# Block transposes through device memory: four loads and a store per tensor, and two more tensors by the same way

## The chip, the cores and the metric

The kernel runs on one core of a Trainium2 chip. The metric is the device time of one execution in microseconds; the kernel before takes 1913.64 us (median of three runs, 1913.54 to 1913.78).

## The reference, cut to what matters

A decoder trunk of two layers on a residual stream x of 256 positions by 2048 channels, all in float32.

- Layer 0: RMS norm, one projection to 12288 + 4096 columns, then 16 heads of stick-breaking attention and 16 heads of dilated attention (head dimension 128, sequence 256), a SiLU gate, and an output projection 4096 to 2048 that is added to x.
- Layer 1: RMS norm, one projection to 16384 columns (q, forget, input, gate), 32 HGRN heads with a 128 x 128 state in chunks, an RMS norm of each head's output, a SiLU gate, and an output projection.

```
a = where(mask, exp(log_sigmoid(z) + tail), 0)            # stick-breaking weights, [queries, keys]
out = a @ v
p = exp(sc - lse);  o = p @ v                             # dilated attention, three strides merged
o = rms_norm(hgrn2(q, f, i, lb), o_gain) * silu(gate)     # HGRN head
x = x + mix @ w_out
```

For the work around the change one thing counts: attention weights come out with queries on the 128 partitions and are needed with keys there, and a HGRN head's output comes out with positions on the partitions and is needed with channels there. Both are transposes.

## The kernel before

**The stream of weights.** All the weights are cut into 640 parts of 128 x 2 x 512 floats (512 KB). Each goes: SP issues a load into a `raw` tile (`Feed.load`, L227, four buffers); ScalarE rounds it to `whi` (L244); VectorE takes the rest, `wlo` (L245); TensorE multiplies 12 times with it (L287 to L289: for two column blocks and two halves of the sequence, `whi` by the activations' high part, `wlo` by the high part, `whi` by the low part). `whi` and `wlo` have four buffers each. A head of either layer takes 8 parts (96 of these weight matmuls), the output projection of a layer 64 parts.

**The heads beside it.** `Side` (L256) holds one generator per head. After each of the 16 steps of a product it advances the generators; `yield n` asks to be called again n steps later. So a head's own work (transposes, scores, softmax, gates) is written into the stream of weights some steps after its product, and lies between the weight matmuls of the next heads.

**What sets the order.** The program is not run in the order in which it is written: a scheduler orders each engine's instructions before the run, by its own costs and by when it takes their inputs to be ready. Each engine then works strictly through its own list. The order rows below are those lists.

**Transposes.** Three kinds stand in the kernel before:
- q, k (and the gate in layer 0), `turn` (L157): `move_blocks` (L143) sends the 4 x 4 blocks of 32 partitions in 16 transfers from the tile `qkp` to the tile `mvp`, each from one group of 32 partitions to another; then one VectorE instruction (L171) transposes all the 32 x 32 blocks. The last head of each layer uses TensorE in place of this (`quick`).
- attention weights, `flip_weights` (L178): three TensorE transposes (`flip`, L136, L140) into a PSUM tile `att`, and a ScalarE copy (L182) to `atk`.
- HGRN outputs (L582): two TensorE transposes into PSUM, read from there by `finish` (L336), which writes the high part (`mixh`, ScalarE, L131) and the low part (`mixl`, VectorE, L132).

**A head of layer 0, step by step**, with the lines that the prediction names: q, k, v and gate are copied from the accumulators (L315, L321); q, k and gate are turned (L171); in a dilated head ScalarE scales k (L411); the gate is computed by VectorE (L327), ScalarE's exponential (L328), VectorE (L329), a reciprocal (L330) and a product (L331); TensorE makes the scores (`products`, L361, L362). A stick-breaking head reads them on VectorE (L371), passes three ScalarE functions (L375 to L377), then VectorE (L378), two scans (L382) and a difference (L383), and ScalarE's exponential (L384). A dilated head reads them with two masked maxima (L420), then has ScalarE's exponentials (L426), sums (L429) and the division (L435). The weights are transposed, TensorE multiplies them by v (`values_by_weights`, L354, L355), VectorE multiplies by the gate (L388 or L439), and `finish` follows.

Of the kernel before, what the change touches and what calls it, by code (L numbers as in the profile page):

```python
# [10 lines left out]
F32 = mybir.dt.float32  # L11
# [20 lines left out]
SG = 4  # L32
# [3 lines left out]
def hybrid_trunk(  # L36
# [23 lines left out]
    psa = ctx.enter_context(tc.tile_pool(name="psa", bufs=4, space=bass.MemoryType.PSUM))  # L60
    psb = ctx.enter_context(tc.tile_pool(name="psb", bufs=4, space=bass.MemoryType.PSUM))
# [74 lines left out]
    def flip(blocks):  # L136

        ps = psb.tile([P, len(blocks) * P], F32, name="att")
        for i, b in enumerate(blocks):
            nc.tensor.transpose(ps[:, i * P : (i + 1) * P], b, ident)  # L140
        return ps

    def move_blocks(moved, src):  # L143


        for a in range(4):
            for b in range(4):
                nc.sync.dma_start(
                    *(
                        v.rearrange("p c t j -> p (c t j)")  # L150
                        for v in (moved[32 * b : 32 * b + 32, a], src[32 * a : 32 * a + 32, b])
                    )
                )
                if b % 2:
                    yield 1

    def turn(flat, part, quick):  # L157


        n = part.shape[2]  # L160
        out = flat.rearrange("p (c t) -> p c t", c=n)
        if quick:
            ps = [flip([part[:, :, c, t, :] for t in range(NT)]) for c in range(n)]
            for c in range(n):
                nc.scalar.copy(out[:, c, :], ps[c])
        else:
            moved = work.tile([P, 4, n, NT, 32], F32, name="mvp", bufs=1)
            yield 2
            yield from move_blocks(moved, part)
            yield 3  # L170
            nc.vector.transpose(  # L171
                out.rearrange("p c (t a j) -> p a (c t) j", t=NT, a=4),
                moved.rearrange("p a c t j -> p a (c t) j"),
            )
            yield 1
        return out

    def flip_weights(w):  # L178

        ps = flip([w[:, j * P : (j + 1) * P] for j in range(3)])  # L180
        at = work.tile([P, 384], F32, name="atk", bufs=2)
        nc.scalar.copy(at, ps)  # L182
        return at
# [181 lines left out]
    def stick_breaking(h, flat, part, v):  # L365
# [18 lines left out]
        nc.scalar.activation(z, z, AF.Exp)  # L384
        yield 12
        at = flip_weights(z)
        yield 3
# [4 lines left out]
    def dilated(h, flat, part, v):  # L392
# [41 lines left out]
        for t in range(NT):  # L434
            nc.vector.tensor_scalar_mul(pr[:, spans[t]], pr[:, spans[t]], ws[:, t : t + 1])  # L435
        yield 8
        at = flip_weights(pr)
        yield 3
# [4 lines left out]
    def blocks(a, n):  # L443
        return a.rearrange("p (b n) -> p b n", n=n)

    def hgrn(h, flat, part, vg):
# [43 lines left out]
        tots = work.tile([P, 2, nb], F32, name="tots")  # L490
# [32 lines left out]
        mm = work.tile([P, 8, 6], F32, name="mm")  # L523
        pr = work.tile([P, 8, 2], F32, name="pr")
# [28 lines left out]
        mx = work.tile([P, 6], F32, name="mx")  # L553
        pr = work.tile([P, 4], F32, name="px")
# [21 lines left out]
        yield 4  # L576
        for t in range(NT):
            nc.vector.scalar_tensor_tensor(
                sg[:, t, :], o[:, t, :], ro[:, t : t + 1], sg[:, t, :], op0=ALU.mult, op1=ALU.mult
            )  # L580
        yield 2
        finish(h, flip([sg[:, t, :] for t in range(NT)]), hg[:, 2:3])  # L582
# [166 lines left out]
```

## Time and profile before

| | |
|---|---|
| median of 3 runs | 1913.64 us |
| the profiled execution | 1914.46 us |
| its span, first to last instruction | 1912.7 us |
| TensorE matmul busy | 1903.1 us (100%) |
| VectorE busy | 1317.7 us (69%) |
| ScalarE busy | 1055.2 us (55%) |
| DMA queue of SP | 144752 packets, 363.11 MB, 60.3% of 16 engines |

The spans of matmuls overlap, so a matmul's cost is read from the distance of the starts around it, not from its duration. The profiled execution lies 0.82 us above the median, and its span 1.76 us below its own time. An engine's idle time matters only where TensorE then waits for it.

### The profile page before, as it was taken

To read this page: it belongs to the slowest core of one execution; us is meant where nothing else is said; L and a number is where in the kernel's file an instruction comes from. 1 tells how busy PE (TensorE), PEld (TensorE's weight loads), DVE (VectorE), ACT (ScalarE), POOL (GpSimd) and SP (SyncE) were. 2 spreads that over 40 slices of the span, in tenths; PEclk is the share of its full clock that TensorE was granted. 3 is DMA by queue.
4 is the path that set the end of the run, shared out by engine and by line. 5 is a ranking of instruction groups with operands and counts; after the bars stand their busy time and mean duration, and the time that the engine had idled before them with its cause. 6 is when DMAs were issued, how large, how long until landed. Compare 5 with 4: busy or idle time off the path is not lost.

```text
span 1912.7 us, 26414 instructions
## 1 busy us (share of the span) xinstructions
PE 1903.1 (100%) x8778; PEld 1586.0 (83%) x8778; DVE 1317.7 (69%) x2598; ACT 1055.2 (55%) x1882; POOL 42.0 (2%) x54
## 2 busy tenths in 40 slices
PE   8999999999999999999999999999999999999999
PEld 7888888888888888888888888888888888888887
DVE  6667777766666666655567777777777777777443
ACT  6555555555555555544456566555565555555332
POOL 0000000000000000000000000000000000000000
PEclk9999999999999999999999999999999999999999
DMA  8666666666666666555565555556555565655664
GB/s 317 197 213 197 198 197 193 196 199 193 194 195 200 195 195 200 177 188 188 187 199 181 182 181 176 174 183 184 172 183 186 178 185 177 186 177 165 198 206 136
DMA packets 145034, 364.82 MB, mean 191 GB/s; under 512 B 27008, under 2 KB 59904, under 8 KB 144896
## 3 DMA queue, kind: packets, MB, share of 16 engines
q1 hardware_dynamic: 144752, 363.11, 60.3%
q8 instruction: 69, 1.13, 0.2%
q14 instruction: 69, 0.57, 0.1%
q10 hardware_dynamic: 144, 0.02, 0.0%
HBM read 340.61 MB, written 2.10 MB: 179 GB/s over the span
## 4 chain that ended last, share of the span: by engine, by line
PE 100%; DMA 0%; ACT 0%; DVE 0%; DVEq 0%; issue 0%
PE acc L287 31%; PE acc L289 31%; PE acc L288 30%; PE att L513 3%; PE att L140 1%; PE att L362 1%; PE att L354 1%; PE att L348 0%; PE att L361 0%; PE att L347 0%; PE att L346 0%; PE att L355 0%; PE att L564 0%; DMA gn<-in_gains 0%; ACT xh L131 0%; ACT whi L244 0%
## 5 line engine op out<-in xcount | busy, mean ns | idle before, releaser
L245 DVE TENSOR_TENSOR wlo<-raw,whi 128x1024 fp32r<-128x1024 f32 (+1 forms) x642 | 781.1, 1217 | 438.0 <-ACT whi L244 409.1
L244 ACT CAST whi<-raw 128x1024 fp32r<-128x1024 f32 (+1 forms) x642 | 672.6, 1048 | 657.8 <-PE acc L289 629.6
L287 PE MATMUL acc<-whi,xh 128*128 128x512 f32 x2048 | 827.9, 404 | 5.9 <-ACT whi L244 5.9
L289 PE MATMUL acc<-whi,xl 128*128 128x512 f32 x2048 | 802.2, 392 | 0.0
L288 PE MATMUL acc<-wlo,xh 128*128 128x512 f32 x2048 | 799.6, 390 | 0.0
L289 PEld LDWEIGHTS acc<-whi,xl 128*128 128x128 f32 x2048 | 385.2, 188 | 83.9
L287 PEld LDWEIGHTS acc<-whi,xh 128*128 128x128 f32 x2048 | 385.9, 188 | 78.7 <-ACT whi L244 5.9
L288 PEld LDWEIGHTS acc<-wlo,xh 128*128 128x128 f32 x2048 | 386.4, 189 | 75.0 <-DVE wlo L245 0.4
L287 PE MATMUL acc<-whi,mixh 128*128 128x512 f32 x512 | 202.3, 395 | 0.0
L289 PE MATMUL acc<-whi,mixl 128*128 128x512 f32 x512 | 199.7, 390 | 0.0
L288 PE MATMUL acc<-wlo,mixh 128*128 128x512 f32 x512 | 199.4, 390 | 0.0
L289 PEld LDWEIGHTS acc<-whi,mixl 128*128 128x128 f32 x512 | 96.2, 188 | 20.1
L288 PEld LDWEIGHTS acc<-wlo,mixh 128*128 128x128 f32 x512 | 96.3, 188 | 19.3
L287 PEld LDWEIGHTS acc<-whi,mixh 128*128 128x128 f32 x512 | 96.2, 188 | 19.0
L315 ACT ACTIVATE qkp<-acc,rstd 128x384 f32<-128x384 f32 (+1 forms) x128 | 68.3, 534 | 41.6 <-PE acc L289 40.3
L171 DVE STREAM_TRANSPOSE qkp<-mvp 128x768 f32<-128x768 f32 (+1 forms) x62 | 52.3, 843 | 39.8 <-DMA mvp<-qkp 39.3
L330 DVE RECIPROCAL sg<-sg 128x256 f32<-128x256 f32 x32 | 56.1, 1752 | 0.5
L321 ACT ACTIVATE pj<-acc,rstd 128x128 f32<-128x128 f32 (+1 forms) x128 | 53.6, 422 | 0.0
L513 PE MATMUL att<-qv,qk 128*128 128x192 f32 x256 | 52.1, 326 | 0.0
L513 PEld LDWEIGHTS att<-qv,qk 128*128 128x128 f32 x256 | 42.5, 190 | 2.4
L212 POOL TENSOR_TENSOR ro<-rv,mhalf 128x2 f32<-128x2 f32 x32 | 23.3, 729 | 801.9 <-DVE pr L526 699.4
L465 DVE TENSOR_TENSOR qk<-qk 128x128 f32<-128x128 f32 x128 | 37.1, 290 | 2.2
(150 smaller groups left out, 1193.6 us busy)
## 6 DMA issues: line engine op xcount, KB each, us to landing
raw<-in_w_odd SPq DMA_DIRECT2D x256, 512.0 KB, 3.6
raw<-in_w_even SPq DMA_DIRECT2D x254, 512.0 KB, 3.9
raw<-in_w_out SPq DMA_DIRECT2D x128, 512.0 KB, 3.4
mvp<-qkp SPq DMA_DIRECT2D x496, 24.0 KB, 3.2
mvp<-qkp SPq DMA_DIRECT2D x496, 16.0 KB, 3.4
xres<-in_xt SPq DMA_DIRECT2D x8, 256.0 KB, 7.1
xres<-in_x SPq DMA_DIRECT2D x4, 512.0 KB, 7.8
out<-xres SPq DMA_DIRECT2D x6, 256.0 KB, 5.1
```

Source lines behind the costliest of these rows:

```text
L171: nc.vector.transpose(out.rearrange("p c (t a j) -> p a (c t) j", t=NT, a=4), moved.rearrange("p a c t j -> p a (c t) j"),)
L212: nc.gpsimd.tensor_tensor(dst, v[:, 0:n], mhalf[:, 0:n], op=ALU.pow)
L244: nc.scalar.copy(hi[:, s, :], half[:, s, :])
L245: nc.vector.tensor_sub(lo[:, s, :], half[:, s, :], hi[:, s, :].bitcast(F32))
L287: nc.tensor.matmul(acc[t], sh[:, k, s], hi, start=(k == 0), stop=False)
L288: nc.tensor.matmul(acc[t], sh[:, k, s], lo, start=False, stop=False)
L289: nc.tensor.matmul(acc[t], sl[:, k, s], hi, start=False, stop=(k == nk - 1))
L315: nc.scalar.activation(part[:, :, :, t, :].rearrange("p b c j -> p c b j"), acc[t][:, 0 : n * P].rearrange("p (c b j) -> p c b j", c=n, b= ...
L321: nc.scalar.activation(rest[:, t, :], acc[t][:, n * P :], AF.Copy, scale=rstd[:, t : t + 1])
L330: nc.vector.reciprocal(sg, sg)
L465: nc.vector.tensor_tensor(o, a, b.broadcast_to(list(o.shape)), op=ALU.mult)
L513: nc.tensor.matmul(ps[:, t, :], kt[:, t * P : (t + 1) * P], qt[t], start=True, stop=True)
```

## The change

`move_blocks` becomes `turn_blocks`: one transfer writes the tile of 128 partitions to device memory, and after three steps four loads, each for 32 partitions, bring the blocks back in moved order; the VectorE transpose of 32 x 32 blocks follows. Attention weights (`turn_weights`) and HGRN outputs take that way too, in tiles `mvw` (moved) and `mvwd` (device memory); only the last head of each layer still uses TensorE. The producers (L384, L435, L578 of before) write the weights and outputs in block order, so that a partition's row is contiguous. The ScalarE copy of the transposed weights goes, since VectorE now writes them to `atk`. To make room, the gate tile `sg` has three buffers in place of four, and some small tiles two in place of three.

```diff
-SG = 4
+SG = 3
+    dram = ctx.enter_context(tc.tile_pool(name="dram", bufs=4, space=bass.MemoryType.DRAM))
-    def move_blocks(moved, src):
-        for a in range(4):
-            for b in range(4):
-                nc.sync.dma_start(
-                    *(
-                        v.rearrange("p c t j -> p (c t j)")
-                        for v in (moved[32 * b : 32 * b + 32, a], src[32 * a : 32 * a + 32, b])
-                    )
-                )
-                if b % 2:
-                    yield 1
+    def turn_blocks(out, src, name):
+        n = src.shape[2]
+        rows = dram.tile([P, 4, n * 32], F32, name=name + "d")
+        nc.sync.dma_start(
+            rows.rearrange("p b x -> p (b x)"), src.rearrange("p b n j -> p (b n j)")
+        )
+        yield 3
+        moved = work.tile([P, 4, n * 32], F32, name=name, bufs=1)
+        v = rows.rearrange("(a i) b x -> i b a x", a=4)
+        for b in range(4):
+            nc.sync.dma_start(moved[32 * b : 32 * b + 32], v[:, b])
+            if b % 2:
+                yield 1
+        yield 3
+        nc.vector.transpose(
+            out.rearrange("p n (a j) -> p a n j", a=4), moved.rearrange("p a (n j) -> p a n j", j=32)
+        )
+        yield 1
...
-    def flip_weights(w):
-        ps = flip([w[:, j * P : (j + 1) * P] for j in range(3)])
+    def turn_weights(w, by32, quick):
         at = work.tile([P, 384], F32, name="atk", bufs=2)
-        nc.scalar.copy(at, ps)
+        if quick:
+            nc.scalar.copy(at, flip([w[:, j * P : (j + 1) * P] for j in range(3)]))
+        else:
+            yield from turn_blocks(at.rearrange("p (n t) -> p n t", n=3), by32, "mvw")
         return at
...
-        nc.scalar.activation(z, z, AF.Exp)
-        yield 12
-        at = flip_weights(z)
-        yield 3
+        w, by32 = weights_tile(False)
+        nc.scalar.activation(
+            by32.rearrange("p b n j -> p n b j"), z.rearrange("p (n b j) -> p n b j", n=3, b=4), AF.Exp
+        )
+        yield 8
+        at = yield from turn_weights(w, by32, False)
...
-        yield 8
-        at = flip_weights(pr)
-        yield 3
+        yield 8 if h == NH - 1 else 3
+        at = yield from turn_weights(w, by32, h == NH - 1)
+        if h == NH - 1:
+            yield 3
...
-        finish(h, flip([sg[:, t, :] for t in range(NT)]), hg[:, 2:3])
+        if h == NH - 1:
+            mo = flip([mo[:, t * P : (t + 1) * P] for t in range(NT)])
+        else:
+            yield from turn_blocks(blocks(mo, P), by32, "mvw")
+        finish(h, mo, hg[:, 2:3])
```

The order that the scheduler makes of it differs far beyond the transposes. Line numbers shift: L287 to L289 become L301 to L303, L245 becomes L259, L171 becomes L161, L361 and L362 become L375 and L376, L354 and L355 become L368 and L369, L371 becomes L385, L420 becomes L436, L330 becomes L344, L439 becomes L460.

**First place: VectorE in a stick-breaking head, from the transposed q, k and gate on.** `wlo` with its number is the split of one weight part; `att` in L371 and L385 are the scores. Before:

```order
L171 STREAM_TRANSPOSE qkp_2383<-mvp_2389 128x4x6x32
L327 TENSOR_SCALAR sg_2555<-qkp_2383 128x256
L245 TENSOR_TENSOR wlo_2546<-raw_2456,whi_2545 128x1024
L329 TENSOR_SCALAR sg_2555<-sg_2555 128x256
L330 RECIPROCAL sg_2555<-sg_2555 128x256
L245 TENSOR_TENSOR wlo_2572<-raw_2478,whi_2571 128x1024
L331 TENSOR_TENSOR sg_2555<-sg_2555,qkp_2383 128x256
L388 TENSOR_TENSOR sg_2353<-att_2581,sg_2353 128x256
L132 SCALAR_TENSOR_TENSOR mixl_103<-sg_2353,mixh_102 128x256
L371 SCALAR_TENSOR_TENSOR wt_2603<-att_2600,strict_89 128x384
L245 TENSOR_TENSOR wlo_2617<-raw_2500,whi_2616 128x1024
L378 SCALAR_TENSOR_TENSOR qv_2605<-wt_2603,qv_2605 128x384
```

Now:

```order
L161 STREAM_TRANSPOSE qkp_2338<-mvp_2388 128x4x6x32
L341 TENSOR_SCALAR sg_2456<-qkp_2338 128x256
L343 TENSOR_SCALAR sg_2456<-sg_2456 128x256
L385 SCALAR_TENSOR_TENSOR wt_2496<-att_2493,strict_91 128x384
L344 RECIPROCAL sg_2456<-sg_2456 128x256
L392 SCALAR_TENSOR_TENSOR qv_2498<-wt_2496,qv_2498 128x384
L345 TENSOR_TENSOR sg_2456<-sg_2456,qkp_2338 128x256
L396 SCALAR_TENSOR_TENSOR qv_2498<-one_88,qv_2498 128x128
L396 SCALAR_TENSOR_TENSOR qv_2498<-one_88,qv_2498 128x256
L259 TENSOR_TENSOR wlo_2523<-raw_2414,whi_2522 128x1024
```

Two splits that stood between the transpose and the scores' reader are gone from there, and the next split stands behind the gate's reciprocal and the scans. On TensorE's list 37 weight matmuls lay between the scores and the first use of the split that follows their reader (heads 3 to 15 before). Now it is 13 in five heads with the rows above and 17 and 21 in one head each; in the other nine heads a split stands right behind the reciprocal, and 17 to 31 matmuls lie between.

**Second place: VectorE in a dilated head, from the product with the gate on.** `att` in L439 and L460 is the weights' product with v of the head before, `att` in L420 and L436 the scores. Before:

```order
L439 TENSOR_TENSOR sg_5129<-att_5327,sg_5129 128x256
L171 STREAM_TRANSPOSE qkp_5135<-mvp_5174 128x4x6x32
L245 TENSOR_TENSOR wlo_5337<-raw_5241,whi_5336 128x1024
L132 SCALAR_TENSOR_TENSOR mixl_103<-sg_5129,mixh_102 128x256
L327 TENSOR_SCALAR sg_5349<-qkp_5135 128x256
L245 TENSOR_TENSOR wlo_5385<-raw_5263,whi_5384 128x1024
L329 TENSOR_SCALAR sg_5349<-sg_5349 128x256
L211 TENSOR_SCALAR rv_5371<-s4_5361 128x4
L330 RECIPROCAL sg_5349<-sg_5349 128x256
L408 TENSOR_SCALAR qkp_5355<-qkp_5355,rr_5370 128x4x32
L331 TENSOR_TENSOR sg_5349<-sg_5349,qkp_5135 128x256
L408 TENSOR_SCALAR qkp_5355<-qkp_5355,rr_5370 128x4x32
```

Now:

```order
L460 TENSOR_TENSOR sg_4955<-att_5164,sg_4955 128x256
L133 SCALAR_TENSOR_TENSOR mixl_105<-sg_4955,mixh_104 128x256
L161 STREAM_TRANSPOSE qkp_4995<-mvp_5101 128x4x6x32
L341 TENSOR_SCALAR sg_5169<-qkp_4995 128x256
L343 TENSOR_SCALAR sg_5169<-sg_5169 128x256
L344 RECIPROCAL sg_5169<-sg_5169 128x256
L436 ISA sp_5239,nm_5237<-att_5234,bias_92 128x128
L436 ISA nm_5237 128x1
L345 TENSOR_TENSOR sg_5169<-sg_5169,qkp_4995 128x256
L436 ISA sp_5239,nm_5237<-att_5234,bias_92 128x256
L436 ISA nm_5237 128x1
L259 TENSOR_TENSOR wlo_5256<-raw_5126,whi_5255 128x1024
```

Before, two splits stand in these rows and a third (with a fourth after the scores' readers) behind them; now the whole chain stands ahead of the next split.

**The same head on TensorE**, from the scores (L361, L362; L375, L376) on, `acc` being the accumulators of the weight stream. Before:

```order
L361 MATMUL att_5413<-qkp_5135 128x128
L362 MATMUL att_5413<-qkp_5135 128x256
L287 MATMUL acc_5332<-whi_5311,xh_100 128x512
L288 MATMUL acc_5332<-wlo_5312,xh_100 128x512
L289 MATMUL acc_5332<-whi_5311,xl_101 128x512
L287 MATMUL acc_5333<-whi_5311,xh_100 128x512
```

Now:

```order
L376 MATMUL att_5234<-qkp_4995 128x256
L302 MATMUL acc_5196<-wlo_5200,xh_102 128x512
L303 MATMUL acc_5196<-whi_5199,xl_103 128x512
L301 MATMUL acc_5195<-whi_5199,xh_102 128x512
L302 MATMUL acc_5195<-wlo_5200,xh_102 128x512
L303 MATMUL acc_5195<-whi_5199,xl_103 128x512
L301 MATMUL acc_5196<-whi_5199,xh_102 128x512
L302 MATMUL acc_5196<-wlo_5200,xh_102 128x512
L303 MATMUL acc_5196<-whi_5199,xl_103 128x512
L301 MATMUL acc_5195<-whi_5255,xh_102 128x512
L301 MATMUL acc_5196<-whi_5255,xh_102 128x512
L302 MATMUL acc_5195<-wlo_5256,xh_102 128x512
```

Before, 43 weight matmuls lay between the scores and the first use of the split behind their readers; now it is 10, and the eleventh uses `wlo_5256`. Thirteen of the sixteen dilated heads have this; the first has 9, the second 2, the last 47. Between the product with v (L369) and the scores stand 13 weight matmuls in these heads. Three transposes per head (L140) are gone from TensorE's list in both kinds of attention heads and two in HGRN heads, 31 heads each.

**Third place: SP in a HGRN head.** `raw` are weight loads, `mvp` the moved q and forget, `mvwd` and `mvpd` the stores to device memory, `mvw` the moved output. Before:

```order
L148 DMA mvp_14361<-qkp_14352 32x128 x4
L233 DMA raw_14340<-in_w_odd 128x1024
L148 DMA mvp_14361<-qkp_14352 32x128
L233 DMA raw_14380<-in_w_odd 128x1024
L148 DMA mvp_14361<-qkp_14352 32x128 x3
L233 DMA raw_14402<-in_w_odd 128x1024
```

Now:

```order
L150 DMA mvwd_11289<-atk_11266 128x256
L150 DMA mvpd_11269<-qkp_11239 128x512
L247 DMA raw_11227<-in_w_odd 128x1024
L157 DMA mvw_11345<-mvwd_11289 32x4x64
L247 DMA raw_11254<-in_w_odd 128x1024
L157 DMA mvp_11317<-mvpd_11269 32x4x128
L247 DMA raw_11277<-in_w_odd 128x1024
L157 DMA mvp_11317<-mvpd_11269 32x4x128 x2
L247 DMA raw_11320<-in_w_odd 128x1024
L157 DMA mvp_11317<-mvpd_11269 32x4x128
```

The loads of q and forget now stand behind the first load of the output of the head before, which waits for that output's store, which waits for VectorE's product (L604, L578 before).

## Rows read from the trace of the kernel before

**Rows 1.** The page: engine busy us (share of span) x instructions.

```profile
PE 1903.1 (100%) x8778; PEld 1586.0 (83%) x8778; DVE 1317.7 (69%) x2598; ACT 1055.2 (55%) x1882; POOL 42.0 (2%) x54
```

**Rows 2.** Waits, whole span: engine line <- releaser: us in total, times, longest.

```profile
ACT whi L244 <- PE acc L289: 629.6, 435, 2.8
```

**Rows 3.** Timeline, TensorE, weights' transposes: start us, us, engine, line, out<-in.

```profile
399.64 0.39 PE L288 MATMUL acc<-wlo,xh 128*128 128x512 f32 x1
...
401.22 0.39 PE L289 MATMUL acc<-whi,xl 128*128 128x512 f32 x1
401.45 0.49 PE L140 MATMUL att<-ident,wt 128*128 128x128 f32 x3
...
402.02 0.39 PE L288 MATMUL acc<-wlo,xh 128*128 128x512 f32 x1
```

**Rows 4.** Timeline, TensorE around the scores of the first head.

```profile
64.46 0.39 PE L288 MATMUL acc<-wlo,xh 128*128 128x512 f32 x1
...
65.57 0.39 PE L287 MATMUL acc<-whi,xh 128*128 128x512 f32 x1
```

**Rows 5.** Timeline, VectorE: the reader of those scores, waiting for them.

```profile
65.54 0.56 DVE L371 SCALAR_TENSOR_TENSOR wt<-att,strict 128x384 f32<-128x384 f32 x1 [2.92 <-PE att L362]
```

**Rows 6.** Groups by line and form, VectorE, 60 to 900 us: busy us, mean ns.

```profile
L245 DVE TENSOR_TENSOR wlo<-raw,whi 128x1024 fp32r<-128x1024 f32 x288 | 351.5, 1221 | 231.2 <-ACT whi L244 215.8 <-DMA mvp<-qkp 15.1
L330 DVE RECIPROCAL sg<-sg 128x256 f32<-128x256 f32 x32 | 56.1, 1752 | 0.5
L171 DVE STREAM_TRANSPOSE qkp<-mvp 128x768 f32<-128x768 f32 x31 | 30.2, 975 | 2.0 <-DMA mvp<-qkp 1.5 <-DMA raw<-in_w_even 0.5
L331 DVE TENSOR_TENSOR sg<-sg,qkp 128x256 f32<-128x256 f32 x32 | 13.4, 420 | 0.0
...
L382 DVE TENSOR_TENSOR_SCAN qv<-one,qv 128x256 f32<-128x256 f32 x16 | 10.7, 666 | 0.0
...
L329 DVE TENSOR_SCALAR sg<-sg 128x256 f32<-128x256 f32 x32 | 9.2, 288 | 1.6 <-ACT sg L328 1.6
...
L371 DVE SCALAR_TENSOR_TENSOR wt<-att,strict 128x384 f32<-128x384 f32 x16 | 8.9, 556 | 4.2 <-PE att L362 2.9
...
L382 DVE TENSOR_TENSOR_SCAN qv<-one,qv 128x128 f32<-128x128 f32 x16 | 6.8, 423 | 0.5
...
L420 DVE CUSTOM_DVE_ANT_0 sp<-att,bias 128x256 f32<-128x256 f32 x16 | 6.7, 420 | 0.0
...
L420 DVE CUSTOM_DVE_ANT_0 sp<-att,bias 128x128 f32<-128x128 f32 x16 | 4.5, 284 | 0.0
```

**Rows 7.** The same, ScalarE.

```profile
L131 ACT ACTIVATE mixh<-sg 128x256 fp32r<-128x256 f32 x32 | 13.4, 419 | 17.0 <-DVE sg L388 15.4 <-DVE sg L439 1.6
...
L411 ACT ACTIVATE qkp<-qkp,qkg 128x256 f32<-128x256 f32 x16 | 8.2, 516 | 0.0
```

**Rows 8.** Timeline of a dilated head, VectorE and TensorE behind the product with v.

```profile
640.27 0.42 DVE L439 TENSOR_TENSOR sg<-att,sg 128x256 f32<-128x256 f32 x1 [1.06 <-PE att L355]
640.30 0.39 PE L288 MATMUL acc<-wlo,xh 128*128 128x512 f32 x1
```

**Rows 9.** Timeline, VectorE, one HGRN head and the start of the next.

```profile
1275.65 0.71 DVE L171 STREAM_TRANSPOSE qkp<-mvp 128x512 f32<-128x512 f32 x1 [2.12 <-DMA mvp<-qkp]
1276.28 1.18 DVE L245 TENSOR_TENSOR wlo<-raw,whi 128x1024 fp32r<-128x1024 f32 x1
...
1287.92 0.35 DVE L578 SCALAR_TENSOR_TENSOR sg<-att,ro,sg 128x128 f32<-128x128 f32 x1 [0.59 <-POOL ro L212]
...
1300.26 0.71 DVE L171 STREAM_TRANSPOSE qkp<-mvp 128x512 f32<-128x512 f32 x1 [1.90 <-DMA mvp<-qkp]
```

**Rows 10.** The tile `mvp`: SP's issues, ns min/median/max, and the landing of its transfers.

```profile
L148 SPq DMA_DIRECT2D mvp<-qkp x992: 507/588/1952, 44.0 to 1718.1; - x199
...
DMA to landing us min/median/max: 1.7/3.3/6.0
```

**Rows 11.** The page: DMA queue of SP: packets, MB, share of 16 engines.

```profile
q1 hardware_dynamic: 144752, 363.11, 60.3%
```

More of the change, by code (lines that the diff above doesn't have):

```diff
@@ L166, in turn, with weights_tile @@
         else:
-            moved = work.tile([P, 4, n, NT, 32], F32, name="mvp", bufs=1)
             yield 2
-            yield from move_blocks(moved, part)
-            yield 3
-            nc.vector.transpose(
-                out.rearrange("p c (t a j) -> p a (c t) j", t=NT, a=4),
-                moved.rearrange("p a c t j -> p a (c t) j"),
+            yield from turn_blocks(
+                flat.rearrange("p (n t) -> p n t", t=P), part.rearrange("p b c t j -> p b (c t) j"), "mvp"
             )
-            yield 1
         return out
-    def flip_weights(w):
-        ps = flip([w[:, j * P : (j + 1) * P] for j in range(3)])
+    def weights_tile(quick):
+        w = work.tile([P, 384], F32, name="qv", bufs=2)
+        if quick:
+            return w, w.rearrange("p (n b j) -> p b n j", n=3, b=4)
+        return w, w.rearrange("p (b n j) -> p b n j", b=4, n=3)
+    def turn_weights(w, by32, quick):
         at = work.tile([P, 384], F32, name="atk", bufs=2)
-        nc.scalar.copy(at, ps)
+        if quick:
+            nc.scalar.copy(at, flip([w[:, j * P : (j + 1) * P] for j in range(3)]))
+        else:
+            yield from turn_blocks(at.rearrange("p (n t) -> p n t", n=3), by32, "mvw")
         return at
@@ L433, in dilated @@
         nc.vector.reciprocal(ws, ws)
-        for t in range(NT):
-            nc.vector.tensor_scalar_mul(pr[:, spans[t]], pr[:, spans[t]], ws[:, t : t + 1])
-        yield 8
-        at = flip_weights(pr)
-        yield 3
+        w, by32 = weights_tile(h == NH - 1)
+        for t, n in ((0, slice(0, 1)), (1, slice(1, 3))):
+            nc.vector.tensor_scalar_mul(
+                by32[:, :, n, :].rearrange("p b n j -> p n b j"),
+                pr[:, spans[t]].rearrange("p (n b j) -> p n b j", b=4, j=32), ws[:, t : t + 1],
+            )
+        yield 8 if h == NH - 1 else 3
+        at = yield from turn_weights(w, by32, h == NH - 1)
+        if h == NH - 1:
+            yield 3
         nc.vector.tensor_mul(sg, values_by_weights(at, v), sg)
@@ L489, in hgrn @@
         times(f8[:, :, 4:8], f8[:, :, 4:8], f8[:, :, 3:4])
-        tots = work.tile([P, 2, nb], F32, name="tots")
+        tots = work.tile([P, 2, nb], F32, name="tots", bufs=2)
         tot = tots[:, 0, :]
@@ L521, in hgrn @@
             nc.vector.copy_predicated(ag[:, :, d0:], hm[:, :, m0 : m0 + n], ps[:, :, c0 : c0 + n])
-        mm = work.tile([P, 8, 6], F32, name="mm")
-        pr = work.tile([P, 8, 2], F32, name="pr")
+        mm = work.tile([P, 8, 6], F32, name="mm", bufs=2)
+        pr = work.tile([P, 8, 2], F32, name="pr", bufs=2)
         t2 = tot.rearrange("p (g a b) -> p g a b", a=2, b=2)
@@ L551, in hgrn @@
             nc.scalar.copy(at[32 * b : 32 * b + 32, :, 32 * b + 32 :], ps[32 * b : 32 * b + 32, :, c0:c1])
-        mx = work.tile([P, 6], F32, name="mx")
-        pr = work.tile([P, 4], F32, name="px")
+        mx = work.tile([P, 6], F32, name="mx", bufs=2)
+        pr = work.tile([P, 4], F32, name="px", bufs=2)
         t2 = tot.rearrange("p (g a) -> p g a", a=2)
@@ L576, in hgrn @@
         yield 4
+        mo = work.tile([P, SEQ], F32, name="atk", bufs=2)
+        if h == NH - 1:
+            by32 = mo.rearrange("p (t b j) -> p b t j", t=NT, b=4)
+        else:
+            by32 = mo.rearrange("p (b t j) -> p b t j", t=NT, b=4)
         for t in range(NT):
             nc.vector.scalar_tensor_tensor(
-                sg[:, t, :], o[:, t, :], ro[:, t : t + 1], sg[:, t, :], op0=ALU.mult, op1=ALU.mult
+                by32[:, :, t, :], blocks(o[:, t, :], 32), ro[:, t : t + 1], blocks(sg[:, t, :], 32),
+                op0=ALU.mult, op1=ALU.mult,
             )
         yield 2
-        finish(h, flip([sg[:, t, :] for t in range(NT)]), hg[:, 2:3])
+        if h == NH - 1:
+            mo = flip([mo[:, t * P : (t + 1) * P] for t in range(NT)])
+        else:
+            yield from turn_blocks(blocks(mo, P), by32, "mvw")
+        finish(h, mo, hg[:, 2:3])
     srcs = []
```

## The prediction

> **What bounds the kernel now.** The page's busy line comes first: TensorE 100 %, VectorE 69 %, ScalarE 55 % [rows 1]. Then the waits: ScalarE's rounding of the next weight part waits 435 times for the last matmul of an older one, 629.6 us in all [rows 2]. So weights arrive early, their buffers are full, and the end is set by TensorE's list alone, one weight matmul every 0.226 us (399.64 to 401.22 are seven of them) [rows 3]. The clock was at its upper level all through, so it is no term. A change gains only by what it takes from TensorE's list and loses only by making TensorE wait. Both have to be priced, the second from the order of VectorE, since each weight part needs its split `wlo`.
>
> **What the change removes.** Three transposes of attention weights cost 402.02 - 401.22 - 2 x 0.226 = 0.348 us of TensorE [rows 3]. 31 heads: 10.8 us. The two transposes of a HGRN head I price at two thirds, 0.23 us (an estimate from the same rows), 31 heads: 7.2 us. In all -18.0 us. ScalarE loses a copy per head, which is worth nothing, since it waits for TensorE anyway [rows 2].
>
> **What it moves: splits behind waits.** VectorE works strictly through its list. Where a reader of scores stands in it ahead of the next split, that split can't start before TensorE has made the scores, and all that lies between the two goes from TensorE's head start. That head start is the number of weight matmuls between the scores and the first use of the split.
>
> *Stick-breaking heads.* In the first head VectorE's reader starts at 65.54 [rows 5], as TensorE begins the second weight matmul behind the scores, at 65.57 [rows 4]. With 13 matmuls between, the fourteenth, which needs the split, would start 12 x 0.226 later: free time 65.57 + 2.71 - 65.54 = 2.74 us. In that time VectorE has to run, in the new order, L385 0.556 (L371 of before), the reciprocal 1.752, L392 0.556 (shape of L385, so its price), L345 0.420, two scans 0.423 + 0.666 and the split 1.221 [rows 6]: 5.594. Neighbours overlap by some 0.08 (0.71 us from 1275.65, but the next starts at 1276.28) [rows 9]; six overlaps leave 5.11, and 0.04 for the last signal (an estimate; starts of VectorE and TensorE are 0.03 apart) [rows 4, 5, 8] 5.15. TensorE waits 5.15 - 2.74 = 2.41 us. Five heads: 12.1. The head with 17 matmuls has 0.90 more, so 1.5; that with 21, 0.6. The other nine have a split right behind the reciprocal: 5.15 less the 2.07 of L392, L345 and the scans and 0.3 of overlaps is under 3.4, against 3.6 free at 17: nothing. Before, 37 matmuls (8.2 us free) covered it all. Sum: 14.2 us.
>
> *Dilated heads.* The chain begins earlier, with L460, which waits for the product with v. In the trace its predecessor starts at 640.27, the second weight matmul behind that product at 640.30 [rows 8]. To the first use of the next split lie 13 weight matmuls, the scores, and 10 more; the scores add 65.57 - 64.46 - 2 x 0.226 = 0.66 us [rows 4]. Free: 0.03 + 22 x 0.226 + 0.66 = 5.66 us. VectorE's chain in the new order: L460 0.420 (as L331, same shape), ScalarE's `mixh` 0.419, `mixl` 0.420 (as L331), the block transpose 0.975, ScalarE's scaling of k 0.516 and exponential of the gate 0.42 (as `mixh`), L343 0.288 (L329 of before), reciprocal 1.752, first maximum 0.284, product 0.420, second maximum 0.420, split 1.221 [rows 6, 7]: 7.555; less six overlaps, plus five signals of 0.04, 7.28. TensorE waits 1.62 us, in 13 heads 21.1. The first such head has one matmul less (1.85), the second eight less (3.43). Sum: 26.4 us. Before, with 43 matmuls and two splits inside the chain, it had over 7 us more.
>
> *HGRN heads.* The weight loads pass in SP's list behind the store of the output. The stall here hangs on a loop that the trace of before doesn't show; it is bounded below as a rival, and at its middle costs nothing.
>
> **What it adds beside other work.** The way through memory adds a store and a landing to each move. In program order eight steps of six matmuls, 8 x 6 x 0.226 = 10.9 us, lie between store and block transpose; two landings of the size of `mvp`'s are 6.6 us at the median, 12.0 at most [rows 10]. Cost taken: nothing, since the median fits; if each way were at its longest, 1.1 us in each of 93 moves that TensorE is near to waiting for, up to 102 us, less what the full buffers hold back [rows 2]. SP issues fewer transfers: sixteen at 0.588 us, 9.4 us a head [rows 10], become two stores and eight loads at most, 5.9. VectorE gets 62 more block transposes of at most 0.71 us (the larger form's) [rows 9], 44 us in 1912.7 of which it is idle 31 %: hidden, except where it stands in the chains above, which name what they hold. Traffic: the moves were 31 x (384 + 256) KB = 19.8 MB; now each byte goes twice, and 31 x (192 + 128) KB more too, 59.5 MB in all. On 363.11 MB at 60.3 % [rows 11] that is some 67 % (estimate): no bound. Three `sg` buffers in place of four: costed at nothing, as a gate is used within a head's turn; if not, it is a wait of VectorE inside the same chains.
>
> Runs of the new loads are 384 and 256 bytes for the attention weights and HGRN outputs. The Trainium skill, page "DMA: Bandwidth & Descriptors", section Specifications, wants 512 bytes or more for full rate, with a read-modify-write below; no run here shows its price, and by it the added 20 MB would take a larger share than the estimate above.
>
> **The sum.** -18.0 + 14.2 + 26.4 = +22.6 us. On the profiled execution, 1914.46 us: 1937.1. That execution lies 0.82 above the median: 1936.
>
> **Rivals.**
>
> *HGRN loop late (slower still).* In SP's list the loads of q and forget stand behind the first load of the output of the head before, which waits for its store, which waits for VectorE's L604. From L604 (1287.92, L578 of before) to the end of the next block transpose's wait (1300.26) [rows 9] there are 12.3 us, less 0.23 for the transposes gone: 12.1. Needed: the store's landing (1.7 to 6.0), six issues that SP makes behind it (0.588 each, three or so), and the last load's landing (3.3, at most 6.0) [rows 10]: from 1.7 + 3.5 + 3.3 + a little = 9.2 at the low to 13.4 with the store at 3.8 and the load at its longest. For: a store to memory is a kind that the trace hardly has, and packets are short. Against: the medians fit with 2 us to spare. It decides once the loop is over 12.1 us: each us over costs 31 us, as the loop closes head by head. At 1 us over: 1936 + 31 = 1967; at 13.4, 1976; the same for the attention moves if they come late.
>
> Of a landing the Trainium skill says, in "DMA: Bandwidth & Descriptors", section Anatomy of one DMA, that some 2 us are fixed, most of it the receipt from the target memory, with device memory the heaviest. The issue-to-landing row of before agrees in size (1.7 at least, with on-chip targets); by it store and load together are over 4 us, inside the bounds above.
>
> *TensorE doesn't wait (faster).* If the stalls are taken up, only the 18.0 us remain: 1914.46 - 18.0 - 0.82 = 1896. For: VectorE is idle 31 % and the waits show buffers full of weights [rows 2]. Against: the split stands behind the waiting reader in the same list, so a full buffer of `raw` or `whi` doesn't help; four buffers of `wlo` would only if splits were ahead, and the order shows which `wlo` the eleventh matmul uses. It decides if durations in the chains are under 5.66 and 2.74 us, 1.6 and 2.4 less than I add up.
>
> TensorE could also run past the late matmul to others whose data lie ready. The Trainium skill ("TensorE: Matmul & The Clock Gate", section Step-by-step) says that only weight loads are pulled ahead and matmuls stay in program order; by that the wait is paid in full. The trace of before has too few waits of TensorE to show it.
>
> *Only one kind of head stalls.* With the stick-breaking heads alone -18.0 + 14.2: 1910, no change; with the dilated alone -18.0 + 26.4: 1922. For: the two chains rest on different waits. Against: both have over 1.6 us of excess.
>
> **How the numbers follow.** Stalls as summed 56 %, HGRN or moves late 26 %, no stalls 10 %, one kind only 8 % (half at 1910, half at 1922). The forecast's own range: half a us more or less in each of the 22 heads that stall, +-11: 1925 to 1947. To hold 8 in 10 it goes down to 1918, which takes in the dilated heads alone and leaves out 1896 and 1910 (14 %), and up to 1976, the upper bound of the HGRN loop, beyond which I leave 6 %. A change under 0.2 % (3.8 us) can't be told from none. Faster: the 10 % and a little of the 1910 case, 0.11. Same: 0.04. Slower: 0.85.
>
> **What the profile after would show.** Right: TensorE has idle time of 30 to 45 us ahead of L302 (released by VectorE's `wlo`), nearly all in the first layer, some 1.6 us a dilated head and 2.4 in five stick-breaking heads; no L140 rows but for the last heads; the second layer shorter by some 7 us. Wrong in the HGRN heads: idle time of TensorE in the second layer, with VectorE's block transposes waiting for `mvp` or `mvw` loads. Wrong altogether: TensorE idle for under 10 us. The forecast fails most easily in the size of the chains, since each tenth of a us counts 22 times, and in the landing of stores, which no row shows.

## The result and the profile after

The changed kernel takes 1959.8 us (median of six, 1952.5 to 1963.2) against 1913.7: a ratio of 1.0234 (1.0213 to 1.0255). It is slower, as forecast, and by twice as much: +46 us for +22. The profiled execution is the shortest of the six, 1952.47 us with a span of 1950.7; its numbers therefore explain 38.0 of the 46 us, and the spread of the executions is part of what has to be explained.

The page first, the lines that answer to [rows 1] and [rows 11], and three of its DMA issues (KB each, median us from issue to landing):

```profile
PE 1904.5 (98%) x8623; PEld 1569.9 (80%) x8623; DVE 1337.5 (69%) x2660; ACT 1036.1 (53%) x1851; POOL 40.0 (2%) x54
...
q1 hardware_dynamic: 186416, 403.72, 66.2%
...
mvpd<-qkp SPq DMA_DIRECT2D x31, 384.0 KB, 5.9
mvp<-mvpd SPq DMA_DIRECT2D x124, 96.0 KB, 4.6
...
mvwd<-qv SPq DMA_DIRECT2D x31, 192.0 KB, 4.8
```

TensorE has 155 instructions less (31 x 5 transposes) and yet a longer span. The traffic is what was estimated (40.6 MB more, 66 %). The landings are not: in layer 0 the stores take 5.9 us (q, k and gate) and 4.8 (weights) and the loads of q, k and gate 4.6, where 3.3 was taken for each. Only the loads of the weights keep it (`mvw`, median 3.3 in layer 0).

The waits, whole span (who waited for what: us in total, times, longest):

```profile
ACT whi L258 <- PE acc L303: 416.8, 270, 3.5
...
ACT whi L258 <- DMA raw<-in_w_even: 104.9, 68, 4.2
...
PE acc L302 <- DVE wlo L259: 30.2, 21, 2.4
...
PEld att L368 <- DVE atk L161: 12.4, 20, 1.4
...
PE acc L301 <- ACT whi L258: 6.0, 2, 5.7
PEld att L375 <- ACT qkp L427: 5.2, 14, 1.4
PE att L368 <- DVE atk L161: 4.2, 9, 1.0
...
PEld att L375 <- DVE qkp L161: 1.2, 1, 1.2
...
PE att L375 <- ACT qkp L427: 1.0, 1, 1.0
...
PE att L375 <- DVE qkp L161: 0.8, 1, 0.8
```

Against [rows 2], ScalarE waits for TensorE 270 times in place of 435, and 68 times for a weight load: in layer 0 the weights no longer come early. TensorE waits 30.2 us for the split, as the order told, and 6.0 us in all for the turned weights and for q and k. (Of the 6.0 us of L301, 5.7 are the start of the program.) PEld is TensorE loading the stationary operand of a matmul; for the scores (L375) and the products with v (L368) these loads wait longer than the matmuls themselves, 12.4 + 5.2 + 1.2 = 18.8 us. Before, the only such row is this:

```profile
PEld att L361 <- issue: 0.2, 1, 0.2
```

All of the loss lies in layer 0. In layer 1 two heads take 49.69 us before and 49.20 now, from the starts of TensorE's first weight matmuls of a head. Before, then after (start us, us):

```profile
1081.31 0.48 PE L287 MATMUL acc<-whi,xh 128*128 128x512 f32 x1
...
1131.00 0.48 PE L287 MATMUL acc<-whi,xh 128*128 128x512 f32 x1
```

```profile
1126.54 0.40 PE L301 MATMUL acc<-whi,xh 128*128 128x512 f32 x1
...
1175.74 0.39 PE L301 MATMUL acc<-whi,xh 128*128 128x512 f32 x1
```

That is 0.245 us a head, 0.23 forecast, some 7.3 us over the layer. Layer 0 is 45.4 us longer (from the first weight matmul, 5.88 and 5.66, to the 3265th, in the output projection, 805.20 and 850.36), where 40.6 - 10.8 = 29.8 was forecast.

**A stick-breaking head.** VectorE from the scores' reader on, one of the five heads with 13 matmuls:

```profile
347.30 0.56 DVE L385 SCALAR_TENSOR_TENSOR wt<-att,strict 128x384 f32<-128x384 f32 x1 [1.75 <-PE att L376]
347.78 1.74 DVE L344 RECIPROCAL sg<-sg 128x256 f32<-128x256 f32 x1
349.56 0.56 DVE L392 SCALAR_TENSOR_TENSOR qv<-wt,qv 128x384 f32<-128x384 f32 x1
350.04 0.42 DVE L345 TENSOR_TENSOR sg<-sg,qkp 128x256 f32<-128x256 f32 x1
350.38 1.00 DVE L396 TENSOR_TENSOR_SCAN qv<-one,qv 128x128 f32<-128x128 f32 x2
351.29 1.20 DVE L259 TENSOR_TENSOR wlo<-raw,whi 128x1024 fp32r<-128x1024 f32 x1
```

The chain takes 351.29 + 1.20 - 347.30 = 5.19 us (5.15 forecast). TensorE's rows at its end:

```profile
352.55 0.61 PE L302 MATMUL acc<-wlo,xh 128*128 128x512 f32 x1 [2.31 <-DVE wlo L259]
352.95 0.63 PE L303 MATMUL acc<-whi,xl 128*128 128x512 f32 x1
353.38 0.63 PE L302 MATMUL acc<-wlo,xh 128*128 128x512 f32 x1
353.81 0.63 PE L303 MATMUL acc<-whi,xl 128*128 128x512 f32 x1
...
355.94 0.52 PE L302 MATMUL acc<-wlo,xh 128*128 128x512 f32 x1
356.30 0.39 PE L303 MATMUL acc<-whi,xl 128*128 128x512 f32 x1
```

It was idle for 2.31 us; the first of these matmuls starts 2.70 us behind the one before it, 2.47 more than the usual 0.227 (2.41 forecast). Then something comes that the forecast lacked: the matmuls stand 0.427 us apart, not 0.227, until 356.3. The granted clock of 2.6 us behind three such waits (stretch, its length, PE busy and instructions, PEclk, DMA share, GB/s):

```profile
303.30:305.90 2.60, 2.48 (x11) 1.00 0.51 150
352.40:355.00 2.60, 2.45 (x6) 0.57 0.56 159
...
484.10:486.70 2.60, 2.49 (x6) 0.50 0.58 187
```

After equal waits of 2.31 us at 303 and 352 us the clock kept its upper level (2.4 GHz) once and fell to the lower (1.2 GHz) once. From L302 behind the wait to the tenth matmul it takes 2.17 us without a fall (303.42 to 305.59) and 3.75 with one: 1.6 us.

**A dilated head.** ScalarE, VectorE and TensorE ahead of the product with v:

```profile
626.77 1.05 ACT L258 CAST whi<-raw 128x1024 fp32r<-128x1024 f32 x1 [0.98 <-DMA raw<-in_w_even]
```

```profile
627.86 1.23 DVE L259 TENSOR_TENSOR wlo<-raw,whi 128x1024 fp32r<-128x1024 f32 x1 [0.19 <-ACT whi L258]
629.00 0.57 DVE L161 STREAM_TRANSPOSE atk<-mvw 128x384 f32<-128x384 f32 x1
630.58 0.42 DVE L460 TENSOR_TENSOR sg<-att,sg 128x256 f32<-128x256 f32 x1 [1.01 <-PE att L369]
...
636.52 1.22 DVE L259 TENSOR_TENSOR wlo<-raw,whi 128x1024 fp32r<-128x1024 f32 x1
```

```profile
629.63 0.70 PE L368 MATMUL att<-atk,pj 128*128 128x256 f32 x2 [0.23 <-DVE atk L161]
...
637.79 0.50 PE L302 MATMUL acc<-wlo,xh 128*128 128x512 f32 x1 [1.16 <-DVE wlo L259]
```

The chain from L460 to the end of the split takes 636.52 + 1.22 - 630.58 = 7.16 us (7.28 forecast). The wait is 1.16 us of idle time, and L302 starts 1.55 us behind the matmul before it, 1.33 more than usual (1.62 forecast): the chain is a little shorter, and TensorE takes a little longer over the scores in between. Ahead of this chain TensorE was already held at the product with v (0.23 idle at 629.63). That hold comes from SP, whose issues of the same stretch read:

```profile
617.04 0.33 SPq L150 DMA_DIRECT2D mvwd<-qv  x1
617.41 0.97 SPq L157 DMA_DIRECT2D mvp<-mvpd  x2
621.34 0.78 SPq L157 DMA_DIRECT2D mvw<-mvwd  x2
622.22 0.38 SPq L247 DMA_DIRECT2D raw<-in_w_even  x1
622.64 0.92 SPq L157 DMA_DIRECT2D mvw<-mvwd  x2
```

From 618.4 to 621.3 SP stands still for the store of the weights to land; the weight load behind it goes out at 622.2, is rounded late at 626.8, split at 627.9, and only behind that split does VectorE transpose the blocks that the product with v needs.

### The profile page after: what moved, and what is told of

It is laid out like the page before. It is cut to its first block, busy times and chain, and to the rows that moved or that the text cites. A ratio compares the mean times of both kernels' runs of the same rounds, so it can differ in the third digit from the quotient of the medians.

```text
span 1950.7 us, 25737 instructions
## 1 busy us (share of the span) xinstructions
PE 1904.5 (98%) x8623; PEld 1569.9 (80%) x8623; DVE 1337.5 (69%) x2660; ACT 1036.1 (53%) x1851; POOL 40.0 (2%) x54
## 4 chain that ended last, share of the span: by engine, by line
PE 82%; DVE 7%; DMA 6%; ACT 3%; issue 2%; SPq 0%; POOL 0%; DVEq 0%; ACTq 0%; POOLq 0%
PE acc L302 25%; PE acc L303 25%; PE acc L301 25%; DMA raw<-in_w_even 3%; PE att L534 3%; DVE wlo L259 2%; DVE sg L344 1%; DMA mvwd<-qv 1%; PE att L368 1%; ACT whi L258 1%; DVE qkp L161 1%; DMA raw<-in_w_out 1%; DMA mvw<-mvwd 0%; PE att L376 0%; DVE qv L396 0%
## 5 line engine op out<-in xcount | busy, mean ns | idle before, releaser
L259 DVE TENSOR_TENSOR wlo<-raw,whi 128x1024 fp32r<-128x1024 f32 (+1 forms) x642 | 778.3, 1216 | 337.1 <-ACT whi L258 336.7
L302 PE MATMUL acc<-wlo,xh 128*128 128x512 f32 x2048 | 807.9, 394 | 30.2 <-DVE wlo L259 30.2
L301 PE MATMUL acc<-whi,xh 128*128 128x512 f32 x2048 | 814.2, 400 | 6.0 <-ACT whi L258 6.0
L303 PE MATMUL acc<-whi,xl 128*128 128x512 f32 x2048 | 804.7, 393 | 0.0
L302 PEld LDWEIGHTS acc<-wlo,xh 128*128 128x128 f32 x2048 | 387.1, 189 | 117.4 <-DVE wlo L259 41.1
L301 PEld LDWEIGHTS acc<-whi,xh 128*128 128x128 f32 x2048 | 386.4, 189 | 82.7 <-ACT whi L258 6.4
L303 PEld LDWEIGHTS acc<-whi,xl 128*128 128x128 f32 x2048 | 386.5, 189 | 82.4
L301 PE MATMUL acc<-whi,mixh 128*128 128x512 f32 x512 | 201.0, 393 | 0.0
L303 PE MATMUL acc<-whi,mixl 128*128 128x512 f32 x512 | 199.6, 390 | 0.0
L302 PE MATMUL acc<-wlo,mixh 128*128 128x512 f32 x512 | 199.5, 390 | 0.0
L303 PEld LDWEIGHTS acc<-whi,mixl 128*128 128x128 f32 x512 | 96.1, 188 | 20.3
L302 PEld LDWEIGHTS acc<-wlo,mixh 128*128 128x128 f32 x512 | 96.2, 188 | 19.8 <-DVE wlo L259 0.2
L301 PEld LDWEIGHTS acc<-whi,mixh 128*128 128x128 f32 x512 | 96.2, 188 | 19.2
L161 DVE STREAM_TRANSPOSE qkp<-mvp 128x768 f32<-128x768 f32 (+1 forms) x62 | 52.2, 841 | 41.5 <-DMA mvp<-mvpd 40.0
L329 ACT ACTIVATE qkp<-acc,rstd 128x384 f32<-128x384 f32 (+1 forms) x128 | 67.4, 531 | 14.6 <-PE acc L303 14.5
L344 DVE RECIPROCAL sg<-sg 128x256 f32<-128x256 f32 x32 | 55.9, 1748 | 0.5
L132 ACT ACTIVATE mixh<-sg 128x256 fp32r<-128x256 f32 x32 | 13.4, 418 | 75.2 <-DVE sg L460 51.4
```

The costliest lines, as they stand in the source:

```text
L161: nc.vector.transpose(out.rearrange("p n (a j) -> p a n j", a=4), moved.rearrange("p a (n j) -> p a n j", j=32))
L259: nc.vector.tensor_sub(lo[:, s, :], half[:, s, :], hi[:, s, :].bitcast(F32))
L301: nc.tensor.matmul(acc[t], sh[:, k, s], hi, start=(k == 0), stop=False)
L302: nc.tensor.matmul(acc[t], sh[:, k, s], lo, start=False, stop=False)
L303: nc.tensor.matmul(acc[t], sl[:, k, s], hi, start=False, stop=(k == nk - 1))
L329: nc.scalar.activation(part[:, :, :, t, :].rearrange("p b c j -> p c b j"), acc[t][:, 0 : n * P].rearrange("p (c b j) -> p c b j", c=n, b= ...
```

## The experiments

The theory: the loss is VectorE's order in layer 0 (splits behind waiting readers), brought about by the attention weights' way through memory; not the transfers as such. The rivals: the transfers (late or too many), or the move of q, k and gate.

**e1, attention weights by TensorE again**, all else as in the changed kernel. The diff below is that of the stick-breaking heads, shortened; the dilated ones are changed alike, with 8 steps in place of 12.

```diff
...
-        yield 8
-        at = yield from turn_weights(w, by32, False)
+        nc.scalar.activation(z, z, AF.Exp)
+        yield 12
+        at = yield from turn_weights(z, None, True)
+        yield 3
...
```

> The changed kernel with one part undone: the attention weights of layer 0 are transposed by TensorE again (with the old distances 12 and 8 steps before it, 3 behind it); q, k, gate and the HGRN outputs still go through device memory. Theory (the way of the attention weights through memory shifts VectorE's order in layer 0, and nothing else costs): layer 0 as in the kernel before, layer 1 shorter by the 31 x 0.245 us that the changed kernel shows there: 1913.7 - 7.6 = 1906, TensorE idle under 1 us behind the start. Rival 1 (four loads and a store for q, k and gate are late): layer 0 stays some 45 us longer, about 1950. Rival 2 (every move through memory shares the loss): in between, about 1925 to 1935.

1907.1 us against 1914.1 (ratio 0.9967, 0.9954 to 0.9979); TensorE's only wait is the start. In this order q, k, gate and the HGRN outputs through memory cost nothing, and the last save what they take from TensorE. Rivals 1 and 2 fall.

**e2, the attention weights alone** (and layer 1) through memory; q, k and gate by the sixteen transfers of before.

```diff
...
+        elif n == 3:
+            moved = work.tile([P, 4, n, NT, 32], F32, name="mvp", bufs=1)
+            yield 2
+            yield from move_blocks(moved, part)
...
```

> The other part undone: in layer 0 q, k and gate go by the sixteen transfers of the kernel before, the attention weights and all of layer 1 go through memory. Theory (the weights' way costs, because SP's list gets longer and weight loads stand behind stores and loads that wait): sixteen issues at 0.588 us and five more per head leave SP even less room, so layer 0 loses at least what it loses in the changed kernel: 1955 to 1985. Rival 1 (the q, k and gate move through memory is what costs): about 1900 to 1910. Rival 2 (the cost is the traffic through device memory, half of which is gone here in layer 0): about 1925 to 1935.

2011.5 us (1.0505, 1.0486 to 1.0524), above the theory's range, with 12 MB less traffic than the changed kernel. Its waits:

```profile
PE acc L324 <- DVE wlo L281: 53.3, 30, 2.0
PE acc L323 <- ACT whi L280: 14.7, 14, 5.6
```

TensorE waits 30 times for the split, about once a head of layer 0, and beside 25 of its 29 waits over 0.9 us the clock is at its lower level (the mean over the span is 0.978). The matmuls in these slow stretches stand some 40 us further apart in all than at 0.227, two thirds of the 62 us of idle time (the start's 5.6 left out). With e1: without the weights' way nothing is lost, with it alone the loss is there. Why it is larger beside the sixteen transfers than in the changed kernel stays open.

**e3, scores later; e4, weights later.** Every transfer stays; only distances change.

```diff
-        yield 3
+        yield 7
         zp = products(qk)
...
-        yield 4
+        yield 8
         z = products(qk)
```

```diff
-        yield 8
+        yield 12
         at = yield from turn_weights(w, by32, False)
...
-        yield 8 if h == NH - 1 else 3
+        yield 8 if h == NH - 1 else 8
```

> The changed kernel with all its transfers; the scores are asked for four steps later (7 and 8 steps behind the gate in place of 3 and 4). In VectorE's list the gate's reciprocal and the tail of the head before then lie apart from the scores' readers: in dilated heads only the two maxima stand between scores and next split, in stick-breaking heads one reciprocal with 11 or 12 weight matmuls free in eleven heads. Theory (order of VectorE): dilated heads stall by nothing, those eleven stick-breaking heads by about 1 us each with refill: 1914 - 18 + 14 = 1910, range 1900 to 1918. Rival (traffic through memory, or SP's weight loads, make the loss wherever the scores stand): no better than 1945.

> The changed kernel with all its transfers; the store of the attention weights comes 4 steps (stick-breaking) and 5 steps (dilated) later. The product with v and the tail of the head move away from the next head's gate and scores: 14 weight matmuls between scores and next split in dilated heads with only the maxima and one product before that split. Theory (order of VectorE): dilated heads stall by nothing, stick-breaking heads as in the run with later scores, about 1 us in nine heads: 1914 - 18 + 14 = 1910, range 1900 to 1920. Rival (lateness of the transfers themselves): starting them later can only make it worse, 1960 or more.

1915.3 us (1.0011, 1.0002 to 1.0021) and 1916.0 (1.001, 1.0001 to 1.002): 44 us of the 46 are gone with the same transfers, so neither their number nor the move of q, k and gate costs this by itself. That the transfers come late for the old distances is not excluded by it; it is part of the account below. What is left is 9.1 and 9.9 us of waits for the split, 0.9 us the longest, 7.6 us of each in ten stick-breaking heads.

**e5, both**, with longer distances: scores 9 and 12 steps behind the gate, weights 8 steps behind the dilated softmax.

```diff
-        yield 3
+        yield 9
         zp = products(qk)
...
-        yield 4
+        yield 12
         z = products(qk)
...
-        yield 8 if h == NH - 1 else 3
+        yield 8 if h == NH - 1 else 8
```

> The changed kernel with all its transfers; scores asked for 9 and 12 steps behind the gate (3 and 4 in the changed kernel), in dilated heads the store of the weights 8 steps behind the softmax (3). In the order, 43 weight matmuls lie between scores and the next split in stick-breaking heads and 47 in nearly all dilated ones, as many as in the kernel before. Theory (order of VectorE is the whole loss): TensorE idle under 2 us behind the start, so the 18 us taken from TensorE are kept: 1914 - 18 = 1896, range 1894 to 1901. Rival (the run with later scores kept a rest of 5 us because the traffic or the transfers' lateness costs some 0.2 us a head wherever the scores stand): 1901 to 1910.

1898.4 us (0.9917, 0.9902 to 0.9932): it beats both kernels. TensorE's waits:

```profile
PE acc L301 <- ACT whi L258: 5.6, 1, 5.6
...
PE acc L302 <- DVE wlo L259: 1.8, 3, 1.1
...
PEld att L368 <- DVE atk L161: 0.6, 1, 0.6
...
PE att L368 <- DVE atk L161: 0.2, 1, 0.2
```

The changed kernel's transfers, bytes and buffers are all in it, in a span shorter by 54 us. Through memory little is lost if the order covers it: 1914.2 - 1898.4 = 15.8 of the forecast's 18 us are kept, and 1.8 more are the waits for the split that are left.

**e6, splits first; e7, weight loads first** in the scheduler's order, distances and transfers untouched.

```diff
-                    nc.scalar.copy(hi[:, s, :], half[:, s, :])
-                    nc.vector.tensor_sub(lo[:, s, :], half[:, s, :], hi[:, s, :].bitcast(F32))
+                    with tc.high_priority(200):
+                        nc.scalar.copy(hi[:, s, :], half[:, s, :])
+                        nc.vector.tensor_sub(lo[:, s, :], half[:, s, :], hi[:, s, :].bitcast(F32))
```

```diff
...
+                self.count += 1
...
-                    nc.sync.dma_start(raw[:, k : k + step, :], src[:, k : k + step, :])
+                    with tc.high_priority(600 if self.count > 40 else 0):
+                        nc.sync.dma_start(raw[:, k : k + step, :], src[:, k : k + step, :])
```

> The changed kernel, its distances and transfers untouched; only the two instructions that split a weight part get precedence in the scheduler's order (200 places). In the order, 13 or more weight matmuls lie between scores and next split in stick-breaking heads, with only the reciprocal before that split, and in dilated heads only the maxima stand before it; the gate and scores wait a little longer instead. Theory (order of VectorE, not the transfers): stick-breaking stalls go to about 0.7 us or less, dilated stalls below 1 us in the heads with 2 to 9 matmuls; 1920 to 1935 in place of 1960. Rival (transfers late or traffic): no change, 1950 to 1962.

> The changed kernel, its distances untouched; only the weight loads get precedence in SP's order (600 places, from the 41st load on), so that they no longer stand behind stores and block loads that wait. Theory (the scheduler puts the splits behind the waiting chain because it takes the weight loads to come late on SP): the stalls of TensorE for the split, 30 us, fall below 5; what comes in their place is the product with v waiting for the block transposes of the weights, whose loads now stand behind weight loads, some 14 us, and waits for the rounded part, some 10 us: 1915 to 1930. Rival (SP's order has no part in it): the stalls for the split stay at 30 us, 1950 to 1962.

e6: 1934.6 us (1.0103, 1.0088 to 1.0119), at the upper end of its range: the order alone moves 25 us. The line numbers are one higher here, and the wait for the split reads:

```profile
PE acc L303 <- DVE wlo L260: 14.0, 25, 1.8
```

In the stick-breaking heads it falls to 0.42 us, as expected; in most dilated heads to 0.8 or less, in one it is 1.8.

e7: 1938.5 (1.0128, 1.0112 to 1.0145), above its range. Its waits:

```profile
PE acc L303 <- ACT pj L337: 13.1, 8, 5.0
PE att L370 <- DVE atk L161: 9.2, 12, 2.9
```

No wait for the split is left, so SP's order does set where the splits stand. But the price comes back elsewhere: the product with v waits 9.2 us (14 expected), and the accumulators are copied late on ScalarE, 13.1 us, which I had not foreseen.

**e8, e9: one kind of head apart.** e8 lengthens the dilated heads' distances alone, e9 the stick-breaking ones', each as in e5, of whose diff e8 has the second and third edit and e9 the first.

> Of the run with all distances longer only the dilated heads' (scores 12 steps behind the gate, weights' store 8 steps behind the softmax); the stick-breaking heads stand as in the changed kernel, row for row on VectorE. It leaves the stick-breaking stalls alone in the program: on top of 1898.4 (no stalls) they cost 14.2 us by the prediction's term, so 1912.6; by the changed kernel's trace, in which the 16 stick-breaking stretches of layer 0 are longer by 15.7 us without three transposes each (5.6), they cost 21.3 us, so 1919.7, and more in executions with more falls of the clock. If the term was right and the excess comes from elsewhere: 1911 to 1915. If idle time costs more than its length (refill, clock): 1917 to 1925.

> The other half: the stick-breaking heads' scores 9 steps behind the gate, the dilated heads as in the changed kernel (10 weight matmuls between scores and next split, the whole chain ahead of it). It leaves the dilated stalls alone: by the prediction's term 26.4 us on top of 1898.4, so 1924.8; by the changed kernel's trace the dilated stretches lose 45.4 + 10.8 - 21.3 = 34.9 us, so 1933.3. The two halves should add: this run and the one with the dilated heads apart, less 1898.4, should give the changed kernel's 1952 to 1963; if they fall short by over 8 us, the two kinds of stall make each other worse.

1920.7 us (1.0035, 1.0023 to 1.0048) and 1930.0 (1.0084, 1.0069 to 1.0099). TensorE waits for the split in e8, then in e9:

```profile
PE acc L302 <- DVE wlo L259: 14.9, 11, 2.3
```

```profile
PE acc L302 <- DVE wlo L259: 17.7, 15, 2.4
...
PE att L368 <- DVE atk L161: 4.6, 6, 1.5
```

Above e5 the stick-breaking stalls cost 22.2 us (14.2 forecast), the dilated ones 31.5 (26.4 forecast). Counted from start to start, e8's trace has 15.0 us more than e5's at the waits for the split and 4.8 behind three falls of the clock. e9's has 18.4 at the waits for the split, 12.6 at the scores and products with v and 1.4 behind one fall. So the excess of the first is mostly the clock, that of the second the late products, and the dilated splits themselves cost less than forecast. The two halves add to 1952.2, the shortest execution of the changed kernel, and miss its median by 7.6, just within the 8 that the expectation allowed.

## Why the prediction was right in kind and short by half

- *Removed, -18.0 us*: right. Layer 1 shows 0.245 us a head and e5 keeps 15.8 in all.
- *Splits behind waits, "+ 14.2 + 26.4"*: right in place and mechanism, 4.7 us too large in sum. The chains measure 5.19 and 7.16 us (5.15, 7.28). Counted from starts, as the prediction counts, the stick-breaking heads lose 14.6 us: 2.47 in exactly five (2.41), 1.6 and 0.7 in the heads with 17 and 21 matmuls (1.5, 0.6). The dilated heads lose 19.0, not 26.4: 1.33 in twelve (1.62 in thirteen) and 2.6 in the second (3.43), while the first shows no such wait. Behind each wait the next matmul follows after 0.337 us in place of 0.227, 2.3 us over the 21 waits, so the splits cost 35.9 us. The Trainium skill ("TensorE: Matmul & The Clock Gate", section Step-by-step) has matmuls in program order; the 21 waits of L302, with other matmuls queued behind, agree.
- *What failed is two terms put at nothing*: "Cost taken: nothing, since the median fits" for the longer way through memory, and "The clock was at its upper level all through, so it is no term." Layer 0 loses 45.4 + 10.8 = 56.2 us in the profiled execution, 15.6 more than the 40.6 of the forecast. With 35.9 for the splits, 20.3 are left. The three falls of the clock cost 1.6, 1.3 and 2.4, in all 5.3. The other 15.0 us lie where TensorE comes to scores and products with v: from the weight matmul ahead of them to the one behind, these stretches take 49.1 us above 0.227 each, 34.1 before and 34.3 in e5. Of the 15.0, 6.0 show as idle time; the rest I put down to waits hidden behind matmuls that last 0.39 us where the next usually follows after 0.227; the weight loads of these products do wait 18.8 us (0.6 in e5). The lateness takes both the way of the weights and the old distances: these stretches are within about 3 us of before in e1 (without that way) and in e3, e4, e5 and e8 (longer distances) and stay at 46.9 in e9, where the dilated heads keep theirs.
- *Signs and range*: the idle time ahead of L302 (30.2 us, 30 to 45 forecast) and the shorter second layer came out as forecast while the loss was double, so these signs don't measure it. That 1959.8 lies between 1918 and 1976 is luck: the upper end was set for a late HGRN loop, which didn't come; the forecast's own 1925 to 1947 misses it.
- *The landing*: 3.3 us taken for store and load; for q, k and gate 5.9 and 4.6 measured, 10.5 together where 10.9 lie between store and block transpose, and for the weights 4.8 and 3.3. SP's stop for the store then delays a weight part, behind whose split the block transpose of the weights stands. The Trainium skill ("DMA: Bandwidth & Descriptors", Anatomy of one DMA) calls device memory the heaviest target, for DMAs that GpSimd issues. Layer 0 agrees in direction (stores 5.9 and 4.8, loads 4.6 and 3.3), layer 1 does not (stores 3.0 and 2.5, loads 4.7 and 3.9). The short runs of 384 and 256 bytes show no price of their own: the queue's share is 66 %, where 67 was estimated without one.
- *HGRN loop late*: wrong. TensorE has no wait in layer 1. *TensorE doesn't wait*: wrong for this order, right for that of e5. *Only one kind stalls*: wrong; e8 and e9 show both.
- *The median*: the six executions differ by 10.7 us, and their mean granted clocks run from 0.996 (1952.5 us) to 0.993 (1963.2). By the clock alone, 0.003 x 1955 is 6 of those 10.7 us; between the profiled one and the median (0.994 and 0.995 in the two executions beside it) it is 2 to 4 of 7.4. Both are rough: the means have three digits, and part of the slow time is idle anyway. What makes the rest stays open.

## What to carry to other kernels

Where each engine works strictly through its list, count the bound engine's instructions between the producer of a value and the first use of what stands behind its reader; a reader moved ahead of the main stream's feed costs the chain behind it, whatever the buffers hold. Beside those stalls, price two things that show little or no idle time: the side products of the same chain, whose weight loads come late (15 us here), and the falls of TensorE's clock behind some of the waits (5 us in the profiled execution). A longer way for data is free only if its consumers are moved away as well: the same transfers cost 46 us at the old distances and saved 16 at new ones.

## What the runs showed of the hardware

Of the changed kernel's waits of about 1.16 and 1.40 us none was followed by a fall of the clock; of the six of 2.3 to 2.4 us three were, for six to ten matmuls each at 0.427 us. In e8, with the same five waits of 2.31 us, it fell at the second, third and fifth; in the changed kernel at the fourth and fifth. In e2 the clock fell beside 25 of 29 waits, there of 1.55 to 2.0 us, while three of 2.0 us passed without a fall. So the length of the wait alone doesn't decide it, and equal kernels come out some us apart. Each of the three falls of the changed kernel cost 1.3 to 2.4 us, from about half the wait to as much.
